# Dots of the matrix memory in buffers of their own, and the order at the ends of two MLPs

## The chip, the cores and the metric

The kernel runs on one core of one Trainium2 chip. The metric is the device time of one execution in microseconds (us); of several runs the median is given. A profiled execution leaves a trace, from which the profile's views are made. Engines in these views: PE is TensorE (PEld its weight loads), DVE is VectorE, ACT is ScalarE, POOL is GpSimd, SP is SyncE, which here issues nearly all DMAs.

## What is computed

A trunk of four residual sub-layers over a sequence of 1024 tokens with 1024 channels, in float32. Cut to what matters here:

```python
for i in range(DEPTH):                      # DEPTH = 2
    mod = c_act @ mod_w[i] + mod_b[i]       # six rows of 1024: shifts, scales, gates
    sh_a, sc_a, g_a, sh_f, sc_f, g_f = [t[:, None, :] for t in jnp.split(mod, 6, axis=-1)]
    h = rms_norm(x) * (1 + sc_a) + sh_a
    y = mla_mixer(h, ...) if i % 2 == 0 else mlstm_mixer(h, ...)
    x = x + g_a * y
    h = rms_norm(x) * (1 + sc_f) + sh_f
    x = x + g_f * conv_ffn(h, ffn_w_up[i], ffn_conv_w[i], ffn_conv_b[i], ffn_w_down[i])
return rms_norm(x, final_norm)

def conv_ffn(h, w_up, conv_w, conv_b, w_down):        # D_FF = 2816
    a, g = jnp.split(h @ w_up, 2, axis=-1)
    a = causal_depthwise_conv3(a, conv_w) + conv_b
    return (jax.nn.gelu(a, approximate=False) * g) @ w_down
```

`mla_mixer` is latent attention with 8 heads. `mlstm_mixer` is the matrix memory, with 4 heads: queries, keys, values, an output gate, and two scalar gates per token and head. The scalar gates give running sums and maxima, from which the decay between tokens comes; the memory is then updated chunk by chunk:

```python
num = inter_w * (C @ q) + ((q @ k.T) * exp(dmat - m)) @ v
C_new = decay * C + (ws * v).T @ k
```

## The kernel before

**Precision and tiling.** Channels lie on the 128 partitions, tokens along the free axis in two halves of 512. Each float32 operand of a large product is split into a high and a low part (type fp32r): ACT copies the source to the high part, DVE or POOL subtracts it from the source to get the low part. One product is then three matmuls, high by high, low by high and high by low (`mm3`, lines 175 to 177). A weight of 128 x 512 or 128 x 1024 is loaded by SP into a raw buffer (`wraw` or `raw`), split into `whi` and `wlo`, and used. `wp` holds four buffers of 1024 columns for the parts (in an MLP eight places of 512) and two called `wraw`.

**Who sets the order.** The program is written as a list of instructions for each engine. A planner (the Tile framework's scheduler) takes them in order of priority, which is their place in the text, and issues on each engine the first that its own model of the chip holds to be ready. So an instruction can float ahead of its place in the text if its inputs and buffers are there, and the order on each engine is fixed when the kernel is built. `tc.high_priority()` moves what is inside it forward; `tc.keep_in_program_order(i)` forbids `i` to overtake the instruction that was written before it on the same engine. On the chip, each engine then works its list strictly in order. `later(n, fn, key)` is a counter in the text: `fn` is written after `n` more `mm3`, or when `need(key)` asks for it.

**Modulation rows.** The six rows of a layer are dots of `mod_w` with silu(c), done on DVE: `mod_dot` (line 198), 128 x 1024 elements with an accumulator, after a load of 512 KB. `mod_steps` is a generator that loads and dots one row block per step, 8 per row; `piece(mods, n)` runs `n` steps. In the matrix memory three rows of the second layer, (1, 2), (1, 4) and (1, 3), are made: 24 steps, two for each of the four parts of the values of the second, third and fourth head (`v_proj`), in raw buffers from `wraw`, each dot written directly behind its load.

**The matrix memory.** First the values of head 0 with the scalar gates' columns (`vp`), then `qk(1)`, the queries and keys of head 1, run while the gates are worked out in four steps, `gates0` to `gates3`, on DVE and ACT with small transposes on PE (`gg`, `gr`, `gp`, `gcol`), written after 2, 16, 20 and 24 `mm3` (`GATES`). `piece(nxt, QK1)` writes 20 `mm3`, and `need(gcol)` then writes the rest. `load_rows` brings the gates' rows back through DRAM; `prep` makes the decayed score matrix `pT` and the weighted queries and keys for a half; `chain` runs the eight chunks, with `po` and `pc` as PSUM tiles. Projections of the next head or of the output gate (`inp`, `vp`) are written between the chunks as cover. After the chain of head 1, `qk(2)` is written, and after that of head 2, `qk(3)`, with `finish`, the head's transposes (`yT`).

**The MLP.** Both products of an MLP, up and down, are cut in halves of the tokens, of the inner channels and of the output rows, with sums and differences of operands and weights, so that seven half products replace eight. The operands are B11, B21, T1, B22, T2, T3 and T4; T1 to T4 are differences, made by DVE and split. The up-projection has 22 groups of 7 steps; a step is four `mm3`. Steps 1 and 2 need only the first half of the normalised input, the others the second. The first four groups (`AHEAD`) run steps 1 and 2 first, because the second half's operands come late; T2, T3 and T4 are written by hooks after steps 7, 8 and 10 of the list (`REST`). `LOOK` says how many steps ahead of its use a weight's preparation is written. Steps 6, 7 and 4 of a group add to the same PSUM bank `A` as step 1, and DVE reads the bank between them (lines 1073, 1080 and 1039). The results go to DRAM (`ud`) and come back as operands of the down-projection, which has three groups of 28 steps; its four U operands take the places of T operands that are done. Hooks at the last steps of the up-projection (`ends`) load these, the residual stream x, and close the pool of the up-projection (`turn`), whose place the second half of the down weights (`raw1`, loaded from `wd`) takes.

**Statistics before an MLP.** `out_proj` sums the squares of x by DVE and ACT. `X_WAIT` `mm3` after the end of a half, PE sums them over the partitions (`st`, line 254), DVE and POOL take the root; `X_RSTD` `mm3` after that PE spreads the result over rows (`rb`, line 266), and the operands can be made (line 915 on).

## Time and profile before

| | |
|---|---|
| median of 3 runs | 2213.28 us |
| lowest and highest | 2211.96 and 2214.94 us |
| the profiled execution, around its span | 2209.6 us |
| its span, first to last instruction | 2207.8 us |
| granted TensorE clock over the span | 0.996 |
| ACT busy | 1045.3 us (47%) |
| POOL busy | 200.5 us (9%) |
| HBM read and written over the span | 221.53 and 44.47 MB |

A row of a group in the profile has the line, engine and operation, then output <- input by the program's names, the shape, the count, and behind the bar the busy time in us and the mean of one in ns; behind the second bar stands the idle time of the engine just before these instructions and what ended it. A row of a timeline begins with the start and the duration in us; a bracket at its end has the idle time before it. A row of the list of waits has the total in us, how often, and the longest. A row of a table of stages has the stage, its length, then busy us and count for PE, PEld, DVE, ACT and POOL, the granted clock, the share of the DMA engines and GB/s. Matmuls are pipelined: one takes about 0.39 us from start to end, and the next starts some 0.23 us after it.

### The profile page before, as it was taken

How to read it: one execution, taken by the hardware profiler on the slowest of the kernel's cores; microseconds unless marked ns; L12 is line 12 of the kernel's file. 1: busy time of each engine (PE TensorE's matmuls, PEld its weight loads, DVE VectorE, ACT ScalarE, POOL GpSimd, SP SyncE). 2: the span in 40 equal slices, each digit the busy share in tenths (PEclk: the TensorE clock that was granted, in tenths of full speed). 3: DMA queues.
4: the chain of work that ended last, by engine and by line, in shares of the span. 5: the costliest groups of instructions: out<-in, count | busy, mean ns of one | idle time of the engine just before them, and what ended most of it. 6: DMA issues, size and time to landing. Idle time of an engine off the chain costs nothing.

```text
span 2207.8 us, 28744 instructions
## 1 busy us (share of the span) xinstructions
PE 2165.6 (98%) x10557; PEld 1817.1 (82%) x10557; DVE 1697.9 (77%) x2753; ACT 1045.3 (47%) x1812; POOL 200.5 (9%) x232
## 2 busy tenths in 40 slices
PE   9999999999999999999999999999999999999998
PEld 7878888787888888778888888988788888877887
DVE  8877788669878776999974754566887777779987
ACT  6456566456444444443353434354554444453335
POOL 0000000000000000242210111010000000022232
PEclk9999999999999999999999999999999999999999
DMA  8512334832444432543133332354233332245122
GB/s 316 156 47 67 94 102 156 278 115 74 151 143 138 134 130 80 191 150 95 51 115 105 102 124 77 114 172 158 68 134 100 110 116 95 78 155 208 45 79 77
DMA packets 105085, 270.50 MB, mean 123 GB/s; under 512 B 12336, under 2 KB 15984, under 8 KB 104944
## 3 DMA queue, kind: packets, MB, share of 16 engines
q1 hardware_dynamic: 104544, 268.28, 36.8%
q8 instruction: 83, 1.36, 0.2%
q14 instruction: 58, 0.48, 0.1%
q10 hardware_dynamic: 400, 0.39, 0.1%
HBM read 221.53 MB, written 44.47 MB: 120 GB/s over the span
## 4 chain that ended last, share of the span: by engine, by line
PE 85%; DVE 8%; DMA 2%; ACT 2%; issue 1%; POOL 0%; SPq 0%; DVEq 0%; POOLq 0%; ACTq 0%
PE pa L177 7%; PE pa L175 7%; PE pa L176 7%; PE pd L175 4%; PE pd L176 4%; PE pd L177 4%; PE sc L677 3%; PE da L175 3%; PE da L177 3%; PE da L176 3%; PE op L175 3%; PE op L177 2%; PE op L176 2%; PE inp L177 2%; PE inp L175 2%; PE db L177 2%
## 5 line engine op out<-in xcount | busy, mean ns | idle before, releaser
L992 ACT ACTIVATE whi<-raw 128x512 fp32r<-128x512 f32 (+1 forms) x252 | 147.5, 607 | 262.3 <-PE pb L176 61.0
L992 ACT ACTIVATE whi<-wsum 128x512 fp32r<-128x512 f32 (+1 forms) x224 | 133.9, 617 | 184.5 <-PE pa L176 61.5
L175 PE MATMUL pa<-T,whi 128*128 128x512 f32 x528 | 206.3, 391 | 5.0 <-DVE g L1080 5.0
L177 PE MATMUL pa<-T,wlo 128*128 128x512 f32 x528 | 206.1, 390 | 3.1 <-DVE wlo L993 3.1
L176 PE MATMUL pa<-T,whi 128*128 128x512 f32 x528 | 205.7, 390 | 0.0
L993 DVE TENSOR_TENSOR wlo<-wsum,whi 128x512 fp32r<-128x512 f32 (+1 forms) x224 | 150.6, 685 | 33.7 <-ACT whi L992 32.2
L993 POOL TENSOR_TENSOR wlo<-raw,whi 128x512 fp32r<-128x512 f32 (+1 forms) x96 | 140.8, 1480 | 382.5 <-ACT whi L992 341.8
L175 PE MATMUL da<-U,whi 128*128 128x512 f32 (+1 forms) x364 | 139.8, 384 | 2.2 <-ACT whi L992 2.2
L176 PE MATMUL da<-U,whi 128*128 128x512 f32 (+1 forms) x364 | 139.2, 382 | 0.0
L177 PE MATMUL da<-U,wlo 128*128 128x512 f32 (+1 forms) x364 | 138.5, 382 | 0.0
L167 ACT ACTIVATE whi<-wraw 128x1024 fp32r<-128x1024 f32 x67 | 70.7, 1058 | 112.7 <-PE op L176 60.2
L993 DVE TENSOR_TENSOR wlo<-raw,whi 128x512 fp32r<-128x512 f32 (+1 forms) x156 | 104.7, 678 | 24.4 <-ACT whi L992 24.4
L175 PEld LDWEIGHTS pa<-T,whi 128*128 128x128 f32 x528 | 99.3, 188 | 28.0 <-DVE g L1080 4.1
L177 PEld LDWEIGHTS pa<-T,wlo 128*128 128x128 f32 x528 | 99.3, 188 | 24.5 <-DVE wlo L993 4.0
L176 PEld LDWEIGHTS pa<-T,whi 128*128 128x128 f32 x528 | 99.3, 188 | 20.4
L1143 DVE TENSOR_TENSOR U<-q,U 128x1024 fp32r<-128x1024 f32 x84 | 108.2, 1306 | 6.0 <-ACT U L1142 5.5
L1032 ACT ACTIVATE ct<-a,cols 128x512 f32<-128x512 f32 x88 | 71.0, 808 | 87.5 <-DVE a L1054 47.8
L168 DVE TENSOR_TENSOR wlo<-wraw,whi 128x1024 fp32r<-128x1024 f32 x67 | 82.4, 1233 | 37.0 <-ACT whi L167 34.9
L177 PE MATMUL db<-U,wlo 128*128 128x512 f32 x264 | 102.7, 390 | 1.7 <-DVE wlo L993 1.7
L175 PE MATMUL db<-U,whi 128*128 128x512 f32 x264 | 103.7, 393 | 0.0
L176 PE MATMUL db<-U,whi 128*128 128x512 f32 x264 | 102.8, 390 | 0.0
L175 PE MATMUL op<-oh,whi 128*128 128x512 f32 x256 | 100.1, 391 | 1.0 <-ACT oh L731 1.0
(378 smaller groups left out, 6078.5 us busy)
## 6 DMA issues: line engine op xcount, KB each, us to landing
raw<-in_wf SPq DMA_DIRECT2D x96, 512.0 KB, 4.1
wraw<-in_w SPq DMA_DIRECT2D x67, 512.0 KB, 3.6
mraw<-in_mod_w SPq DMA_DIRECT2D x56, 512.0 KB, 3.6
ud<-ct SPq DMA_DIRECT2D x88, 256.0 KB, 2.3
q<-ud SPq DMA_DIRECT2D x88, 256.0 KB, 4.1
raw<-in_wd SPq DMA_DIRECT2D x32, 512.0 KB, 5.7
pa<-in_mod_w SPq DMA_DIRECT2D x24, 512.0 KB, 3.6
x<-xd SPq DMA_DIRECT2D x48, 256.0 KB, 4.4
```

The source lines that it names most:

```text
L167: act.activation(hi, raw, AF.Copy)
L168: dve.tensor_tensor(lo, raw, hi.bitcast(F32), ALU.subtract)
L175: pe.matmul(ps, lh, rh, start=first, stop=False, skip_group_check=more)
L176: pe.matmul(ps[:, 0:rl.shape[-1]], lh, rl, start=False, stop=False, skip_group_check=more)
L177: pe.matmul(ps, ll, rh, start=False, stop=last, skip_group_check=more)
L677: pe.matmul(ps[:, cs], a[:, qs if n < 3 else qrs_], b[:, cs], start=n == 0, stop=n == 4)
L992: act.activation(hi, src, AF.Copy)
L993: eng.tensor_tensor(lo, src, hi.bitcast(F32), ALU.subtract)
L1032: act.activation(t, a[:, 2:], AF.Identity, bias=col(f"cb{l}", m), scale=cw(m, 2))
L1143: dve.tensor_tensor(lo, w, hi.bitcast(F32), ALU.subtract)
```

## The change

- `GATES` goes from (2, 16, 20, 24) to (2, 18, 22, 26).
- `mod_steps` now writes every dot one step after its load, and pinned behind what was written before it on DVE; before, this held for the steps without a row `c` of their own, and the matrix memory's dots stood directly behind their loads. Their raw buffers are two of a pool of the matrix memory (`MRAWS`), no longer `wraw`. The steps move from `v_proj` of heads 1 to 3 to `qk(2)` and `qk(3)`: two and one in each half of each projection, 12 for each head.
- `X_WAIT` and `X_RSTD` of the second half go from 4 to 3.
- In the first eight steps of an MLP the weights are written 7 ahead instead of 5.
- In the first four groups the order 5, 4, 5, 4 of two pairs becomes 5, 5, 4, 4.
- `out` of step 4 (the product with the gate, and its store) gets high priority.
- In the first group of the down-projection the low parts of the weights of B11 and B21 are made by DVE instead of POOL.
- The last step 4 of the up-projection moves behind the first two steps of the down-projection, and with it, two places later, `turn` and the loads of x for the first half.

```diff
-GATES = (2, 16, 20, 24)
+GATES = (2, 18, 22, 26)
...
-AHEAD, LOOK, RAWS = 4, 5, 5
-X_WAIT, X_RSTD = (12, 4), (8, 4)
+AHEAD, LOOK, RAWS, MRAWS = 4, (7, 5), 5, 2
+X_WAIT, X_RSTD = (12, 3), (8, 3)
...
                 nc.sync.dma_start(raw, mod_w[l, j * 8 + k])
-                if c is None:
-                    yield
-                    tc.keep_in_program_order(mod_dot(l, j * 8 + k, raw))
-                else:
-                    mod_dot(l, j * 8 + k, raw, c)
-                    yield
+                yield
+                tc.keep_in_program_order(mod_dot(l, j * 8 + k, raw, c))
...
         def p4(g, w):
             prod(g["A"], w, "T4", False)
-            out(g, 0, g["t1"], g["A"])
+            with tc.high_priority():
+                out(g, 0, g["t1"], g["A"])
...
-            seq += [(k, g) for g in pair] if k != (5, 4) else [(5, b[0]), (4, a[0]), (5, b[1]), (4, a[1])]
+            seq += [(k, g) for g in pair] if k != (5, 4) else [(5, b[0]), (5, b[1]), (4, a[0]), (4, a[1])]
...
-                return wop(weights(g, p, 0)[op == "B21"], pool)
+                return wop(weights(g, p, 0)[op == "B21"], pool if g else dve)
...
-        hook(ends[4], turn)
-        hook(ends[4], lambda: load_x_tiles(0))
+        hook(ends[4] + 2, turn)
+        hook(ends[4] + 2, lambda: load_x_tiles(0))
...
+        e = ends[4]
+        seq[e:e + 3] = [*seq[e + 1:e + 3], seq[e]]
         ws = []
         for i, (_, run_) in enumerate(seq):
-            while len(ws) < len(seq) and len(ws) <= i + LOOK:
+            while len(ws) < len(seq) and len(ws) <= i + LOOK[i >= 2 * AHEAD]:
...
             for hf in range(2):
-                yield from in_steps(u, hf, lambda ps: qk_evac(ps, t, hf, scale))
+                for n, _ in enumerate(in_steps(u, hf, lambda ps: qk_evac(ps, t, hf, scale))):
+                    if hd > 1:
+                        piece(mods, 2 - n)
+                    yield
...
             split_ps(va[0][:, 2 * t2:2 * t2 + 2, 0:256], va[1][:, 2 * t2:2 * t2 + 2, :], ps3)
-            piece(mods, 2)
             yield va
...
-                     lambda: wp.tile([P, 1024], F32, tag="wraw", bufs=wraws, name=nm("mraw")), crow2)
+                     lambda: pm.tile([P, D], F32, tag="mraw", bufs=MRAWS, name=nm("mraw")), crow2)
```

## The prediction

> **What bounds the kernel now.** I read the first part of the page, and then the table of stages of 50 us.
>
> ```profile
> span 2207.8 us, 28744 instructions
> ...
> PE 2165.6 (98%) x10557; PEld 1817.1 (82%) x10557; DVE 1697.9 (77%) x2753; ACT 1045.3 (47%) x1812; POOL 200.5 (9%) x232
> ...
> 500.00:550.00 50.00, 47.58 (x209) 38.77 (x208) 49.71 (x71) 31.67 (x48) 0.10 (x1) 1.00 0.23 68
> ...
> 650.00:700.00 50.00, 50.00 (x223) 41.40 (x222) 40.29 (x66) 22.56 (x38) 0.30 (x3) 1.00 0.45 151
> ...
> 1200.00:1250.00 50.00, 45.41 (x280) 39.10 (x279) 38.73 (x102) 22.31 (x59) 7.75 (x9) 1.00 0.49 153
> ```
>
> TensorE is busy 2165.6 of 2207.8 us, so a change that takes away no matmul can win at most the 42.2 us in which it idles. In a stage without holes it does 223 matmuls in 50 us, one per 0.225 us; one weight block against one operand block, three matmuls (`mm3`), takes 0.67 us, and a step of the MLP (four of them) 2.7 us. In each row the first pair after the length is PE, the third DVE. Two kinds of hole show: stages where DVE is nearly full (49.71 of 50), and the matrix memory's first head (45.41), where DVE is not full and something is late. The diff touches both kinds. It removes no matmul and adds none.
>
> **The matrix memory.** Three holes, by the list of waits between 1186 and 1240 us, and the DVE timeline at two of them:
>
> ```profile
> PE po L177 <- DVE pT L1405: 2.3, 1, 2.3
> PE gr L1567 <- DVE crow L1563: 2.1, 1, 2.1
> ...
> PE po L175 <- ACT pT L1404: 0.9, 1, 0.9
> ...
> 1198.22 1.21 DVE L198 SCALAR_TENSOR_TENSOR mraw<-mraw,crow 128x1024 f32<-128x1024 f32 x1
> ...
> 1199.37 0.41 DVE L1563 TENSOR_TENSOR_SCAN crow<-crow 32x128 f32<-32x128 f32 x1
> ...
> 1200.76 0.17 DVE L1575 COPY mprow<-mend 1x28 f32<-1x28 f32 x1
> ...
> 1219.57 1.21 DVE L198 SCALAR_TENSOR_TENSOR mraw<-mraw,crow 128x1024 f32<-128x1024 f32 x1
> ...
> 1222.29 0.68 DVE L1405 TENSOR_TENSOR pT<-crow,pT 128x512 fp32r<-128x512 f32 x1
> ```
>
> L198 is the dot of a modulation row. In the text it belongs to the second head's values, but the planner has floated it forward: it stands directly ahead of the scan that the gates wait for, and between 1219.57 and 1222.29 (there are two) ahead of the low part of pT that `po` waits for. After the change no dot is written before the third head's queries, and each is pinned behind the DVE instruction traced before it, so none can stand here.
>
> - Hole of 2.1 (`gr`): without the dot the scan starts at 1198.22, 1.15 us sooner; GATES puts `gr` two `mm3` later, 2 x 0.67 = 1.35 us that TensorE works meanwhile. 1.15 + 1.35 = 2.5 > 2.1: it goes. The third and fourth gate step move as well, but the end of `piece(nxt, QK1)`, 20 `mm3`, already brings the rest; `gp` now follows `gr` after two `mm3` instead of four. What it needs, L1575, ends at 1200.93, 1.15 us after the scan's end at 1199.78 with `gr` between them; two `mm3` take 1.35, so I cost that at nothing, and at 1.15 if they did not cover it.
> - Hole of 2.3 (pT low): 1222.29 - 1219.57 = 2.72 us of dots go. 2.72 > 2.3: it goes.
> - Hole of 0.9 (pT high): the chain is sooner by 1.15 at the scan and by up to 1.35 at `gp`, 2.5 in all, and TensorE arrives 2.1 sooner. What is left of the gain is about 0.4; I take 0.5, the middle of the ends 0 and 0.9.
>
> Sum: -(2.1 + 2.3 + 0.5) = **-4.9 us**; ends -5.3 and, if the scheduler floats other DVE work into the freed places so that only the hole at `gr` goes, about -2.0.
>
> What it adds: the same 24 dots and 24 loads, 12 for each of the third and fourth head, in `qk`. The stage of the third head's queries and keys:
>
> ```profile
> 1300.00:1324.00 24.00, 24.00 (x124) 20.43 (x123) 13.67 (x20) 4.29 (x6) 1.56 (x1) 1.00 0.54 175
> ...
> L198 DVE SCALAR_TENSOR_TENSOR mraw<-mraw,crow x6: 1212/1223/1226, 1299.9 to 1315.1; 128x1024 f32<-128x1024 f32 x6
> ...
>   DMA mraw<-in_mod_w: 14.0, 12
> ```
>
> TensorE is full there, DVE 13.67 of 24 with six dots in it already; six more are 6 x 1.22 = 7.3 us, within the 10.3 free. (The last row counts what DVE waited for landings ahead of all 24 dots.) The loads go through two buffers of their own, so the weights' loads no longer queue behind dots for `wraw`. Cost: nothing, as long as TensorE's projection covers it (the second rival prices it without that cover).
>
> **Start of each MLP.** PE and DVE timelines of the first one, ACT's last square, a table of one stage, and two rows of the list of waits of the whole span:
>
> ```profile
> 485.56 0.63 ACT L233 ACTIVATE sq<-x 128x512 f32<-128x512 f32 x1
> ...
> 487.24 0.28 PE L254 MATMUL st<-ones,ssq 128*128 128x1 f32 x2
> ...
> 489.12 0.16 DVE L258 TENSOR_SCALAR var<-st 128x4 f32<-128x4 f32 x1 [2.45 <-PE st L254]
> 492.06 0.69 DVE L1054 TENSOR_TENSOR a<-a,pb 128x512 f32<-128x512 f32 x1 [2.78 <-PE pb L177]
> ...
> 514.29 2.35 DVE L922 TENSOR_TENSOR T<-o,T 128x1024 fp32r<-128x1024 f32 x2
> ...
> 519.48 0.39 PE L175 MATMUL pa<-T,whi 128*128 128x512 f32 x1
> ...
> 528.67 0.47 PE L175 MATMUL pa<-T,whi 128*128 128x512 f32 x1 [0.87 <-DVE g L1080]
> ...
> 530.92 0.50 PE L177 MATMUL pa<-T,wlo 128*128 128x512 f32 x1 [1.55 <-DVE wlo L993]
> ...
> 492.10:553.70 61.60, 59.18 (x261) 48.38 (x260) 61.31 (x84) 40.30 (x60) 0.10 (x1) 1.00 0.25 76
> ...
> PE pa L175 <- DVE g L1080: 5.0, 4, 1.7
> PE pa L177 <- DVE wlo L993: 3.1, 2, 1.5
> ```
>
> DVE starves (2.45 and 2.78 us) until the statistics of the second half arrive, then works 61.31 of 61.60 us, and TensorE loses 0.87 + 1.55 = 2.4 us inside that stretch. So the stretch is DVE's, and its start decides. X_WAIT and X_RSTD bring the statistics one `mm3` sooner and the turn to rows one more: L915, whose work opens the stretch, starts 2 x 0.67 = 1.35 us sooner. The inputs allow it: the last square ends at 486.19, and the statistics would start at 487.24 - 0.67 = 486.57. In a full stretch each microsecond sooner is one less of waiting, up to 2.4: -1.35 per MLP, **-2.7 us** for two: the waits of the second kind are 3.1 in two places, so the second MLP shows the same.
>
> The rest here adds no operation. LOOK of 7 writes three weights ahead of T2's operands, about 2.1 us of DVE (three low parts and a sum, each near the 678 ns of the group L993 below); T2 is done at 516.64 and first read at 519.48, so 2.8 us of slack hides it, and without it up to 2.1 would show. The order (5, 5, 4, 4) gives TensorE something else to do while T4 is late, but step 5's weight comes off the same full DVE at the same time as the weight that step 4 waited for. I take 0; bounds -1.05 (the rest of the 2.4) and +1.0 per MLP.
>
> **End of each MLP's up-projection.** The list of waits between 880 and 1000 us, the table of one stage, the groups of the low parts on DVE and on POOL, and DVE groups in 890:960 against 600:850:
>
> ```profile
> PE pa L175 <- DVE g L1080: 1.7, 1, 1.7
> PE da L175 <- ACT whi L992: 1.1, 2, 0.6
> PE db L177 <- DVE wlo L993: 0.8, 1, 0.8
> ...
> 903.60:959.20 55.60, 53.09 (x229) 41.87 (x228) 55.45 (x67) 21.17 (x30) 10.42 (x6) 1.00 0.58 198
> ...
> L993 DVE TENSOR_TENSOR wlo<-raw,whi 128x512 fp32r<-128x512 f32 (+1 forms) x156 | 104.7, 678 | 24.4 <-ACT whi L992 24.4
> ...
> L993 POOL TENSOR_TENSOR wlo<-raw,whi 128x512 fp32r<-128x512 f32 x64 | 103.3, 1628 | 295.7 <-ACT whi L992 255.0 <-DVE U L1143 35.3 <-PE da L177 5.3
> ...
> L1033 DVE SCALAR_TENSOR_TENSOR ct<-a,cols,ct 128x512 f32<-128x512 f32 x2 | 3.0, 1488 | 0.0
> ...
> L1039 DVE TENSOR_TENSOR ct<-ct,g 128x512 f32<-128x512 f32 x2 | 2.3, 1168 | 0.0
> ...
> L1033 DVE SCALAR_TENSOR_TENSOR ct<-a,cols,ct 128x512 f32<-128x512 f32 x27 | 20.2, 747 | 3.5 <-ACT ct L1032 3.5
> ...
> L1039 DVE TENSOR_TENSOR ct<-ct,g 128x512 f32<-128x512 f32 x13 | 9.0, 689 | 0.2
> ```
>
> The hole of 1.7 is the last step 4, which waits for DVE to take step 7's result out of the same bank. The change puts two steps of the down-projection (5.4 us) ahead of it, so this wait goes. But DVE works 55.45 of 55.60 us from 903.6 to 959.2, through that hole and the next (the 0.8 on `db`): TensorE that arrives 1.7 us sooner at `db` finds DVE where it was. What is late next is that low part, by 1.7 more. Unless DVE's work there shrinks, nothing is won.
>
> Does it? Eight low parts per MLP (B11 and B21 of the first group) go from POOL to DVE: 8 x 0.68 = 5.4 us more, about half of it after 903.6. Against it, DVE operations are long where POOL works beside them: L1033 by 0.74 us and L1039 by 0.48, about 0.6 a part, 8 x 0.6 = 4.8 us that go away, again spread over both halves. 5.4 - 4.8 = +0.6, half of it in the full stretch. That is small beside the rest of the stretch, and I take **0** per MLP; bounds +2.7 (no relief, half of 5.4) and -3.6 (all three waits go).
>
> The Trainium skill, page "SBUF — State Buffer", section "Who interferes with whom", has a DVE instruction with two SBUF inputs and a GpSimd instruction that reads SBUF exclude each other for the whole instruction. By that rule eight POOL parts could hold DVE for 8 x 1.63 = 13 us, and moving them would free 7.6 us per MLP. By the rows the trace agrees only in part: 0.6 us a part, not 1.63; the third rival carries the rest.
>
> The moved `turn` and `load_x_tiles(0)`: eight x loads, and behind them on SP's queue the wd loads for T1.
>
> ```profile
> 921.23 2.22 SPq L1155 DMA_DIRECT2D raw<-in_wd  x4
> ...
> 928.50 1.28 DVE L1166 TENSOR_TENSOR wsum<-raw 128x512 f32<-128x512 f32 x2
> ...
> raw<-in_wd SPq DMA_DIRECT2D x32, 512.0 KB, 5.7
> ```
>
> Before, the wd loads start at 921.23, as soon as the x loads are out; the first lands about 921.2 + 5.7 = 926.9, used at 928.5: 1.6 us of slack. Step 4 is moved by two steps, 5.4 us, less the 1.7 that it no longer waits and what the planner runs ahead of it already: at most 3.7 us later, against 1.6 of slack. I take nothing, because part of the two steps does run ahead of it, at worst +2.1 per MLP. `out` of step 4 at high priority is one DVE operation sooner and keeps the store, and with it `turn`, from drifting.
>
> **Sum.** -4.9 - 2.7 + 0 = -7.6 us. The profiled execution took 2209.6 us around its span of 2207.8, and would take 2202.0; the median of the runs shown is 2213.28, 3.7 above it, so I give **2205.7**.
>
> **Rivals.**
> 1. DVE's full stretches take it back: the moved low parts bring no relief (+2.7 per MLP), while the starts and the memory give what I forecast. -4.9 - 2.7 + 5.4 = -2.2, 2211.1 us: not to be told from no change. For it: 55.45 of 55.60. Against: the long L1033 and L1039.
> 2. Slower: the pinned dots hold DVE. A dot whose row has not landed stops everything behind it on DVE: the low parts of weights, then `prep` and `chain` of the next head. Before, 12 such waits took 14.0 us, 1.17 each. If all 24 wait so, DVE needs 12 x (1.22 + 1.17) = 28.7 us beside the 6 us of other work in a stage of 24 us: 10.7 over per head, 21.4 in all. Should all of it reach TensorE: -7.6 + 21.4 = +13.8, 2227.1 us. It decides from about 12 us on. Against it: before, those waits fell where TensorE stayed full (24.00 of 24.00), and a row has a buffer to land in while the other is worked on.
> 3. POOL's release pays in full: the three waits at each transition go (1.7 + 1.1 + 0.8 = 3.6 per MLP, 7.2 in all): 2205.7 - 7.2 = 2198.5 us. For it: 1488 against 747 ns. Against: the 1.1 is two waits on ACT's whi, not on POOL.
> 4. The scheduler floats other work into the freed places, the memory gives -2.0 alone: 2208.6, inside the first case's range.
>
> **Chances.** Forecast with rival 4: 0.55 (2202 to 2209). Rival 1: 0.21. Rival 2: 0.08. Rival 3: 0.16. Forecast and rival 3 lie below 2208.9, so faster by over 0.2% (about what a measurement of this kernel can tell from no change): 0.71. Within: rival 1, 0.21. Slower: rival 2, 0.08. The range takes in rivals 3 and 1 and leaves out rival 2: 2198.5 to 2212.
>
> **What would show it.** Memory right: no L198 on DVE before about 1290, and the list of waits at 1186 to 1240 without `gr` <- L1563 and `po` <- L1405. Start right: L915 begins 1.35 us sooner after the last `op` matmul, and the two waits together are near 1 us instead of 2.4. Transition right: the wait on L1080 is gone and those on `db` and `da` have grown by about as much, with DVE still full. Wrong: DVE waits for `mraw` and TensorE for DVE in the third and fourth head (rival 2), or transitions without any wait (rival 3).

## The result, and the profile after

| kernel | median us | executions | ratio to the kernel before, 95% interval |
|---|---|---|---|
| before, beside it | 2214.11 | 6 | |
| changed | 2196.92 | 6 | 0.9923 [0.991, 0.9936] |
| changed, measured again | 2196.77 | 5 | 0.9932 [0.992, 0.9945] |

The change is faster by 17.2 us, 0.77%. The forecast was 2205.7, with a range of 2198.5 to 2212: the time lies below the range. The sign was right, and the gain is more than double the forecast 7.6 us.

The first rows of the changed kernel's page, and from its list of TensorE's waits over the whole span (total us, how often, longest) those rows of 1 us and more that belong to the places of the prediction:

```profile
span 2194.9 us, 28739 instructions
...
PE 2164.6 (99%) x10557; PEld 1818.9 (83%) x10557; DVE 1692.5 (77%) x2769; ACT 1049.7 (48%) x1812; POOL 175.2 (8%) x216
```

```profile
PE da L177 <- DVE wlo L989: 2.0, 2, 1.0
...
PE pd L175 <- ACT whi L988: 1.9, 2, 1.0
...
PE po L176 <- DVE C L1475: 1.6, 3, 0.6
PE po L175 <- ACT C L1474: 1.6, 3, 1.0
...
PE db L175 <- ACT whi L988: 1.3, 2, 0.6
```

Line numbers are up to 4 off those of before: L989 was L993, L1035 was L1039, L1140 was L1143, L1475 was L1473. Before, the list was led by `pa` <- `g` L1080 with 5.0 us in four places; that wait is gone everywhere. The span is 12.9 us shorter than that of the one profiled execution before, but the medians are 17.2 apart. The row to keep in mind for what follows is DVE: it is busy 1692.5 us against 1697.9, although it made 16 more low parts.

**Memory, after.** Waits of TensorE from 1186 to 1240, then DVE (three rows) and TensorE (one) at the scan:

```profile
PE po L175 <- ACT pT L1406: 0.7, 1, 0.7
PE po L175 <- ACT C L1474: 0.3, 1, 0.3
PE po L176 <- DVE C L1475: 0.3, 1, 0.3
```

```profile
1195.05 0.28 DVE L1564 TENSOR_TENSOR crow<-crow 32x128 f32<-32x128 f32 x1
1195.36 0.41 DVE L1565 TENSOR_TENSOR_SCAN crow<-crow 32x128 f32<-32x128 f32 x1
...
1197.59 0.17 DVE L1577 COPY mprow<-mend 1x28 f32<-1x28 f32 x1
```

```profile
1198.11 0.17 PE L1582 MATMUL gp<-ident,mprow 1*32 1x1 f32 x1
```

No dot stands ahead of the scan: it starts where its input ends (1195.33). Neither `gr` nor `po` <- pT low is in the list, and `gp` runs 0.35 us after its input is there, without a wait of its own. Before, the list had two small rows more than the prediction showed:

```profile
PE po L176 <- DVE C L1473: 0.8, 1, 0.8
PE po L175 <- ACT C L1472: 0.6, 1, 0.6
```

With these, five waits of 6.7 us have become three of 1.3.

**Start and end of an MLP, after.** DVE's first row of the full stretch; the same stretches as before in the tables of stages; DVE's groups from 890 to 960:

```profile
491.81 2.35 DVE L911 TENSOR_TENSOR x<-x,rb 128x1024 f32<-128x1024 f32 x2 [2.46 <-PE rb L262]
```

```profile
492.10:553.70 61.60, 60.50 (x264) 48.77 (x263) 61.31 (x85) 42.23 (x63) 0.10 (x1) 1.00 0.25 88
```

```profile
903.60:959.20 55.60, 53.96 (x236) 43.76 (x235) 55.16 (x71) 20.55 (x30) 2.98 (x2) 1.00 0.60 206
```

```profile
L989 DVE TENSOR_TENSOR wlo<-raw,whi 128x512 fp32r<-128x512 f32 x13 | 8.8, 685 | 0.0
...
L1029 DVE SCALAR_TENSOR_TENSOR ct<-a,cols,ct 128x512 f32<-128x512 f32 x2 | 1.5, 745 | 0.0
L1035 DVE TENSOR_TENSOR ct<-ct,g 128x512 f32<-128x512 f32 x2 | 1.4, 685 | 0.0
```

Both stretches are still DVE's (61.31 of 61.60, 55.16 of 55.60), yet TensorE gets through 264 instead of 261 matmuls in the first and 236 instead of 229 in the second. At the start, L911 (L915 before) begins 6.4 us after the end of the last `op` matmul, before 8.0: 1.6 sooner, where 1.35 was forecast. The two waits of 2.4 us have become two of 1.1 (`pd`, on whi and on wlo; 1.2 in the second MLP). At the end, POOL works 2.98 us in the stretch, not 10.42, and the `ct` operations that took 1488 and 1168 ns take 745 and 685, the usual time. TensorE's waits there went from 3.6 to 1.8 us (3.5 to 1.8 in the second MLP): the one on `g` is gone, and the two others of before, 1.9 us, have become three of 1.8:

```profile
PE da L177 <- DVE wlo L989: 1.0, 1, 1.0
PE db L175 <- ACT whi L988: 0.6, 1, 0.6
PE da L175 <- DVE x L294: 0.2, 1, 0.2
```

### The profile page after: what moved, and what is told of

Its sections match the earlier page's. It is cut to its first block, busy times and chain, and to the rows that moved or that the text cites. A ratio compares the mean times of both kernels' runs of the same rounds, so it can differ in the third digit from the quotient of the medians.

```text
span 2194.9 us, 28739 instructions
## 1 busy us (share of the span) xinstructions
PE 2164.6 (99%) x10557; PEld 1818.9 (83%) x10557; DVE 1692.5 (77%) x2769; ACT 1049.7 (48%) x1812; POOL 175.2 (8%) x216
## 4 chain that ended last, share of the span: by engine, by line
PE 84%; DVE 9%; DMA 2%; ACT 2%; issue 2%; POOL 0%; SPq 0%; DVEq 0%; POOLq 0%; ACTq 0%
PE pa L175 7%; PE pa L177 7%; PE pa L176 7%; PE sc L673 3%; PE pd L177 3%; PE pd L175 3%; PE pd L176 3%; PE db L175 3%; PE db L176 3%; PE db L177 3%; PE op L175 3%; PE op L176 3%; PE op L177 3%; PE da L175 2%; PE da L176 2%; PE da L177 2%
## 5 line engine op out<-in xcount | busy, mean ns | idle before, releaser
L989 DVE TENSOR_TENSOR wlo<-wsum,whi 128x512 fp32r<-128x512 f32 (+1 forms) x224 | 151.5, 692 | 33.0 <-ACT whi L988 31.6
L989 POOL TENSOR_TENSOR wlo<-raw,whi 128x512 fp32r<-128x512 f32 (+1 forms) x80 | 116.3, 1467 | 401.2 <-ACT whi L988 398.7
L989 DVE TENSOR_TENSOR wlo<-raw,whi 128x512 fp32r<-128x512 f32 (+1 forms) x172 | 116.1, 681 | 24.9 <-ACT whi L988 24.9
L1140 DVE TENSOR_TENSOR U<-q,U 128x1024 fp32r<-128x1024 f32 x84 | 102.7, 1239 | 10.3 <-ACT U L1139 9.8
L175 PE MATMUL inp<-h,whi 128*128 128x512 f32 x256 | 100.9, 395 | 0.0
```

Of the source, the lines that this page charges most:

```text
L175: pe.matmul(ps, lh, rh, start=first, stop=False, skip_group_check=more)
L989: eng.tensor_tensor(lo, src, hi.bitcast(F32), ALU.subtract)
L1140: dve.tensor_tensor(lo, w, hi.bitcast(F32), ALU.subtract)
```

## Experiments

Ratios are to the kernel before, measured beside it on the same chip, with a 95% interval; "us" is (ratio - 1) x 2213. Where a stage is compared, the time between the same two TensorE instructions (by their count, 10557 in all) is taken from both traces, so that the rest of the kernel doesn't matter. This table is worked out from the traces in that way; it gives each stage's time less that of the first profiled execution of before, in us.

| kernel | MLP 1 start (486 to 870) | MLP 1 end (870 to 1090) | memory (1180 to 1300) | memory (1300 to 1450) | MLP 2 start (1560 to 1930) | MLP 2 end (1930 to 2110) |
|---|---|---|---|---|---|---|
| before, again | +1.4 | +0.2 | +2.2 | +1.0 | -0.2 | -0.2 |
| memory alone | +1.6 | 0 | -5.1 | +2.7 | -1.6 | 0 |
| ends alone | +1.3 | -1.9 | +1.5 | 0 | -0.1 | -2.8 |
| low parts alone | +1.5 | -0.7 | +0.7 | +2.7 | 0 | -2.8 |
| order of the ends alone | 0 | +1.0 | +2.1 | +0.7 | -1.6 | +0.1 |
| starts alone | -1.0 | 0 | +1.4 | +0.6 | -2.6 | 0 |
| statistics alone | -1.5 | +0.1 | +1.9 | +0.8 | -3.1 | 0 |
| changed | -1.0 | -2.9 | -5.2 | +0.7 | -2.6 | -3.0 |
| changed, again | -1.0 | 0 | -5.8 | 0 | -2.7 | -1.3 |
| no POOL parts, weights 9 ahead | -1.4 | -4.5 | -5.8 | +0.8 | -3.0 | -5.3 |

Stages that an edit doesn't touch differ by up to 2.7 us between executions: by half-clock stretches of TensorE, to which the section on the hardware comes back, and from 1300 to 1450 also by TensorE's wait on C, which was 0.6 us in the first profile of before, 1.4 in the second and 1.5 in that of the low parts alone. In the start of the second MLP the execution of before that all are compared with has a stretch of half clock at 1598, so up to 1.7 us of the -1.6, -2.6 and -3.1 there are that stretch.

### The kernel before, once more

No edit.

> The kernel before, unchanged, profiled once more. The profiled execution of before took 2209.6 us, 4.5 below the median of its six runs, while that of the change lies 0.3 from its median. Theory A: that execution was a short one of the same program; this one has a span near 2212 and the difference to the first is spread over the whole span or lies in one place that waits for DMA. Rival B: a profile costs nothing and the span is 2208 again; then the runs' 17.2 us hold about 4 us that no profiled execution shows.

Measured 2212.24 us, ratio 1.000 [0.999, 1.001]. Its profiled execution has a span of 2213.1, 5.3 above the one that the prediction was made from: that one was at the fast end of the kernel's own spread. As far as the table shows, the difference lies in the places where this execution has half-clock stretches and the first has none (531, 1204 and 1228), and in the wait on C.

### The three parts

The memory: the hunks on `GATES`, `mod_steps`, `qk`, `v_proj` and `mods`. The ends: the hunks on `d_w`, `hook(ends[4] + 2, ...)` and `seq[e:e + 3]`. The starts: those on `LOOK`, `X_WAIT`, the order 5, 5, 4, 4 and `out`. Each is the diff of the change cut to these lines, the first of each:

```diff
-GATES = (2, 16, 20, 24)
+GATES = (2, 18, 22, 26)
...
-                return wop(weights(g, p, 0)[op == "B21"], pool)
+                return wop(weights(g, p, 0)[op == "B21"], pool if g else dve)
...
-X_WAIT, X_RSTD = (12, 4), (8, 4)
+X_WAIT, X_RSTD = (12, 3), (8, 3)
```

> Only the matrix memory's part: the dots in two buffers of their own, pinned and moved to the third and fourth head's queries and keys, and the gates' places. Theory: the holes at the gates and at the first two products of the chain go, 5.5 us by the matmul counts of the two traces (1150 to 1250 us); ratio 0.9975. Rival: the part also carries what the runs show beyond the traces (17.2 against 12.9); then 9 to 10 us, ratio 0.9955.

> Only the end of each up-projection: the low parts of the first group on DVE, the last step 4 two steps later with its hooks. Theory: POOL's release of DVE is worth about 1 us a part against 0.68 that the part costs, DVE's busy time falls by about 5 us in all, and each MLP wins 2.8 us: 5.6, ratio 0.9975. Rival (my prediction): DVE stays full and gives the hole back at the next product, 0 to 1 us, ratio 1.000.

> Only the start of each MLP: statistics sooner, weights 7 ahead, the order 5, 5, 4, 4, step 4's product at high priority (this last one acts in all groups). Theory: 1.0 us per MLP, 2.1 in all, ratio 0.999. Rival: the high priority shortens other waits on DVE in the groups' steady state too, 4 us or more, ratio 0.998.

| part | median us | ratio | us | forecast |
|---|---|---|---|---|
| memory | 2207.72 | 0.9977 [0.9968, 0.9986] | -5.1 | -4.9 |
| ends | 2206.66 | 0.9969 [0.9958, 0.9981] | -6.9 | 0 |
| starts | 2209.02 | 0.9982 [0.9972, 0.9991] | -4.0 | -2.7 |

Each interval is 4 to 5 us wide. The three add up to -16.0, within that of the whole change's -17.2, so nothing shows that the parts touch each other. Of the 9.6 us that the forecast missed, 6.9 are the ends.

### The ends: POOL or the order

The first run moves the low parts only, the second the last step 4 with `turn` and the x loads only.

```diff
-                return wop(weights(g, p, 0)[op == "B21"], pool)
+                return wop(weights(g, p, 0)[op == "B21"], pool if g else dve)
```

```diff
-        hook(ends[4], turn)
-        hook(ends[4], lambda: load_x_tiles(0))
+        hook(ends[4] + 2, turn)
+        hook(ends[4] + 2, lambda: load_x_tiles(0))
...
+        e = ends[4]
+        seq[e:e + 3] = [*seq[e + 1:e + 3], seq[e]]
```

> Before, with one part alone: the low parts of B11 and B21 of the down-projection's first group on DVE instead of POOL (8 an MLP); turn, the x loads and the last step 4 stay where they were. It splits the 6 to 7 us that the two edits at the end of the up-projection gave together. Theory POOL: each part that leaves POOL frees about 1.0 us of DVE and costs it 0.68, so DVE's busy time falls by about 5 us in the span, and the edit alone gives -3 to -6 us: about 2208 to 2210. The wait of step 4 on DVE (g, 1.7 us an MLP) stays. Theory order (the one of the prediction): the relief is 0.6 a part, DVE's busy time stays within 1 us, and the edit alone gives 0, within 1.5 us of the kernel before.

> Before, with the other half of that pair alone: the last step 4 of the up-projection behind the first two steps of the down-projection, with turn and the x loads two places later; the low parts stay on POOL. Theory POOL: DVE is as full as before, so TensorE only meets it later; the wait on g goes and those on wlo and whi at da and db grow by about 1.7 us an MLP: 0, within 1.5 us. Theory order: the 1.7 us an MLP are won whatever POOL does: -3.4 us. If the two edits need each other, both runs give less than half of the 6.9 us of the pair.

Low parts alone: 2209.61, ratio 0.9986 [0.9976, 0.9995], -3.1 us. Order alone: 2214.45, 1.001 [1.0, 1.002], +2.2. Both: -6.9. The engine rows of the pages of, in this order, the kernel before again, the order alone, the low parts alone and both:

```profile
PE 2171.0 (98%) x10557; PEld 1821.2 (82%) x10557; DVE 1698.9 (77%) x2753; ACT 1045.3 (47%) x1812; POOL 200.5 (9%) x232
```

```profile
PE 2165.5 (98%) x10557; PEld 1816.5 (82%) x10557; DVE 1699.3 (77%) x2753; ACT 1048.1 (47%) x1812; POOL 199.0 (9%) x232
```

```profile
PE 2170.2 (98%) x10557; PEld 1823.0 (82%) x10557; DVE 1693.7 (77%) x2769; ACT 1049.4 (47%) x1812; POOL 177.2 (8%) x216
```

```profile
PE 2168.2 (98%) x10557; PEld 1822.2 (83%) x10557; DVE 1692.4 (77%) x2769; ACT 1046.3 (47%) x1812; POOL 176.2 (8%) x216
```

DVE has 16 instructions more in the last two (2769 against 2753) and is busy 5 to 7 us less. One low part on DVE takes 0.68 us, so 16 add 10.9; DVE's other work has become 16 to 18 us shorter, 1.0 to 1.1 us for each part that left POOL. The order does nothing to DVE.

The place where this reaches TensorE is the wait on `g`. DVE takes step 6's result out of the bank at L1073 and step 7's at L1080, which is when `g` is there. Before, on DVE and then on POOL:

```profile
904.17 2.21 DVE L1141 TENSOR_TENSOR q<-q,q 128x1024 f32<-128x1024 f32 x1
906.31 1.78 DVE L1033 SCALAR_TENSOR_TENSOR ct<-a,cols,ct 128x512 f32<-128x512 f32 x1
...
909.82 0.68 DVE L1080 TENSOR_TENSOR g<-g,pa 128x512 f32<-128x512 f32 x1
```

```profile
904.02 3.53 POOL L993 TENSOR_TENSOR wlo<-raw,whi 128x512 fp32r<-128x512 f32 x2 [2.39 <-ACT whi L992]
```

With the low parts alone:

```profile
907.19 0.68 DVE L993 TENSOR_TENSOR wlo<-raw,whi 128x512 fp32r<-128x512 f32 x1
907.80 1.22 DVE L1141 TENSOR_TENSOR q<-q,q 128x1024 f32<-128x1024 f32 x1
908.93 0.75 DVE L1033 SCALAR_TENSOR_TENSOR ct<-a,cols,ct 128x512 f32<-128x512 f32 x1
...
910.83 0.68 DVE L1080 TENSOR_TENSOR g<-g,pa 128x512 f32<-128x512 f32 x1
```

Two parts on POOL make two DVE operations 2.0 us longer. One low part (0.6 us from start to start) takes their place there, and L1034 (0.7) now comes after L1080, so that `g` is there 4.9 us after L1073 starts instead of 7.0 (4.8 instead of 7.0 in the second MLP). The wait on `g` is gone with the low parts alone, which neither theory expected. TensorE's time from 903.6 to 930, and over the same place in the second MLP, is 1.9 to 2.0 us shorter in the profiles of the low parts alone, of both, and in the two of the changed kernel: 3.9 us for the two MLPs.

What the order does alone is in its waits from 880 to 1000 us:

```profile
PE da L175 <- DVE ct L1039: 1.6, 1, 1.6
PE db L177 <- DVE wlo L993: 1.4, 2, 0.9
PE da L175 <- ACT whi L992: 1.1, 2, 0.6
```

The wait on `g` is gone, and a wait of the same 1.6 us has come in its place: `da` takes the bank that step 4's `out` reads, and now waits for that read. It is the prediction's "TensorE that arrives 1.7 us sooner at `db` finds DVE where it was". The theory called POOL gave the order alone 0, within 1.5 us; +2.2 is beyond that on the slow side. Together the two win more than the sum of both alone (-0.9). That the two edits need each other isn't shown: the intervals are 4 to 5 us wide, and in the second MLP the profile of the low parts alone wins as much as that of both (-2.8).

### No low part on POOL

```diff
-                return wop(weights(g, p, 0)[op == "B21"], pool if g else dve)
+                return wop(weights(g, p, 0)[op == "B21"], dve)
...
-                return wop(weights(g, p, 1)[1], pool)
+                return wop(weights(g, p, 1)[1], dve)
...
-                       pool if op == "T3" else dve)
+                       dve)
```

> The changed kernel with no low part of the down-projection on POOL at all: the 80 that were left there go to DVE. It asks whether the relief of about 1.0 us a part holds for the others too. Relief 1.0 everywhere: DVE's busy time falls by 80 x 0.3 = 24 us, to about 1668, and since most of these parts lie where TensorE is full, the time falls by 0 to 3 us: 2194 to 2197. Relief only where DVE has no slack of its own (POOL shares little of its time with a busy DVE): DVE's busy time rises by up to 80 x 0.68 = 54 us, to about 1745, and the stages where DVE has 2 to 5 us free fill up: 2197 to 2205.

2192.9 us, ratio 0.991 [0.9891, 0.9928]. From 880 to 1000 us, TensorE has no wait left that the list shows. Neither expectation on DVE held, and the time is below both their ranges: DVE's busy time rose to 1701.0, by 8.5, so 80 more parts cost it about 0.1 each, a relief near 0.57 a part.

The relief can also be read off operation by operation: each DVE operation that overlaps a low part on POOL, less the median of the same operation in the fastest version without POOL parts (below). So counted, the 96 parts of before lengthen DVE by 50 us, 0.52 a part, and the 80 of the changed kernel by 35 to 36. The eight parts that the change moves lengthen it by 4.6 to 5.6 us in each MLP, 0.58 to 0.70 a part. Most of the rest of the 1.0 to 1.1 above is the parts that stayed, which lengthen DVE less than before: in the first MLP 15.4 to 17.0 us instead of 18.6, in the second 10.5 to 11.1 instead of 13. Why they do isn't shown.

How POOL holds DVE up shows best in the second run of the changed kernel, on DVE and on POOL, and in the group of the same operation from 880 to 1080 in the fastest version:

```profile
986.41 1.65 DVE L1140 TENSOR_TENSOR U<-q,U 128x1024 fp32r<-128x1024 f32 x1
987.98 2.31 DVE L1138 TENSOR_TENSOR q<-q,q 128x1024 f32<-128x1024 f32 x1
...
991.91 2.31 DVE L1138 TENSOR_TENSOR q<-q,q 128x1024 f32<-128x1024 f32 x1
```

```profile
983.42 9.72 POOL L989 TENSOR_TENSOR wlo<-raw,whi 128x512 fp32r<-128x512 f32 x5 [2.78 <-ACT whi L988]
```

```profile
L1138 DVE TENSOR_TENSOR q<-q,q 128x1024 f32<-128x1024 f32 x10 | 12.1, 1214 | 0.2 <-DMA q<-ud 0.2
```

Five low parts in a row on POOL, 1.94 us each, and the difference that takes 1214 ns takes 2310. Behind it TensorE waits 1.5 us for DVE's x (L294), and that execution's first MLP end won nothing (the table above): what the other parts on POOL take back there differs from execution to execution. The Trainium skill, page "SBUF — State Buffer", section "Who interferes with whom", has the two engines exclude each other on a shared port; a delay of 1.1 us on one operation beside POOL parts of 1.94 agrees with it in kind, while the mean over the 96 parts of before, 0.52, doesn't reach a part's length.

### The memory without GATES

All hunks of the memory but the first; against the run with the memory alone:

```diff
-GATES = (2, 18, 22, 26)
+GATES = (2, 16, 20, 24)
```

> Before, with the matrix memory's dots moved to the queries and keys of the third and fourth head, pinned, in two buffers of their own, and GATES left at (2, 16, 20, 24). The forecast's steps: the scan starts 1.15 us sooner, so of the hole of 2.1 us at gr 0.95 stays; the holes of 2.3 and 0.9 at pT stay gone or nearly so. By that it gives -3.5 us, against -5.1 with GATES. Rival: the dots are all of it and GATES nothing, because the planner, with no dot to float there, puts gr where its inputs are: -5, no wait on L1563. Other rival: the planner floats other DVE work into the freed place: the hole at gr stays near 2, -2 to -3 in all.

2207.93 us, ratio 0.9984 [0.9974, 0.9994], -3.5. Its list of waits from 1180 to 1240:

```profile
PE gr L1565 <- DVE crow L1561: 0.9, 1, 0.9
PE po L175 <- ACT pT L1402: 0.8, 1, 0.8
```

The step was 2.1 - 1.15 = 0.95, and 0.9 is there, so the dots are the main thing and `GATES` takes the rest. Both rivals fall by this list; the medians alone, 1.6 us apart, couldn't tell.

### The start: statistics or order

```diff
-X_WAIT, X_RSTD = (12, 4), (8, 4)
+X_WAIT, X_RSTD = (12, 3), (8, 3)
```

```diff
-AHEAD, LOOK, RAWS = 4, 5, 5
+AHEAD, LOOK, RAWS = 4, (7, 5), 5
...
-            seq += [(k, g) for g in pair] if k != (5, 4) else [(5, b[0]), (4, a[0]), (5, b[1]), (4, a[1])]
+            seq += [(k, g) for g in pair] if k != (5, 4) else [(5, b[0]), (5, b[1]), (4, a[0]), (4, a[1])]
...
-            out(g, 0, g["t1"], g["A"])
+            with tc.high_priority():
+                out(g, 0, g["t1"], g["A"])
```

> Before with the statistics of the second half sooner (X_WAIT and X_RSTD 3 instead of 4) and nothing else of the start. Theory of the prediction: DVE's full stretch opens 1.35 us sooner in each MLP, and the two holes at its end (1.0 and 1.7 us) shrink by that much together: -2.7 us, about 2209.5. Rival: the holes at 529 to 531 are a matter of what DVE does just ahead of the weight, not of when the stretch began; then the stretch opens sooner, the holes stay within 0.3 us of 1.0 and 1.7, and the time is the same within 1 us.

> Before with the other part of the start: weights 7 ahead in the first eight steps, the order 5, 5, 4, 4, and out at high priority; the statistics as they were. Theory of the prediction: 0, within 2 us, the holes at 529 to 531 stay about 2.7 together. Rival: the order alone takes the hole of 1.7 us away (TensorE has a step 5 to do while step 4's operand is late), so the two together fall to about 1.1 and the time by 3.4 us; then the part with the statistics should give nothing beside it.

Statistics alone: 2208.98, ratio 0.9982 [0.9973, 0.9991], -4.0 us. The other part alone (weights 7 ahead, the order, `out` at high priority): 2209.06, 0.9988 [0.9979, 0.9997], -2.7. Waits from 495 to 560, first with the statistics, then with the order:

```profile
PE pd L175 <- ACT whi L992: 0.9, 1, 0.9
```

```profile
PE pd L177 <- DVE wlo L993: 0.9, 1, 0.9
PE pd L175 <- ACT whi L992: 0.4, 1, 0.4
```

Of the 2.4 us of before, 0.9 is left by the one and 1.3 by the other; with both, 1.1. The theory of the full stretch holds for the statistics: the stage is 1.5 us shorter in the first MLP (forecast 1.35). The order alone takes the two waits to 1.3, near what the rival named (1.1) and not the prediction (2.7); its stage is 0.6 us shorter in each MLP. Beside the statistics it wins nothing: the stage is 1.0 shorter with both, 1.5 with the statistics alone. The medians can't order the two parts, since their intervals overlap.

### Filling a hole

To see whether a hole costs more than its length, matmuls that nobody reads were put into the one at `gr`: 16, and then 8, because one of float32 took two passes of 0.109 us and 16 held `gr` up.

```diff
         ps = px("gr")
+        for _ in range(FILL):
+            tc.keep_in_program_order(pe.matmul(ps[:, 0:P], ident, ident, start=True, stop=True))
```

> Before with 16 matmuls of 128 x 128 of the identity with itself, written into the bank of gr ahead of its transposes, so that TensorE works through most of its hole of 2.1 us at 1200 (16 x 0.109 = 1.7 us). The result of these is overwritten; nothing else is changed, and the hole's end stays where DVE's scan puts it. Theory clock: the hole costs more than its length, because the granted clock is halved for about 3.4 us behind a window with much idle time (1.7 us of loss, in about three of four executions of before there); filled, there is no half clock between 1198 and 1210 in the profile, the mean granted clock rises by about 0.0005, and the time falls by about 1.3 us although 16 matmuls were added. Theory idle time: only the length of the hole counts; the time is the same, or up to 0.3 us longer, and the mean clock is that of before, 0.9935.

> As the run with 16 filling matmuls ahead of gr, with 8: of float32, one took two passes of 0.109 us, so 16 took 3.6 us and held gr up by 1.4; 8 take 1.75 and end inside the hole of 2.1. Theory clock: no half clock between 1198 and 1210 in the profile, and the median 0.5 to 1.3 us below the kernel before, with a mean clock 0.0003 to 0.0007 above its 0.9935. Theory idle time: the time is that of before within 0.5 us, and so is the mean clock.

2214.68 us, ratio 1.0011 [1.0002, 1.002], with 16; 2212.45, 0.9999 [0.999, 1.0007], with 8. In both profiles the clock stays full through 1200 to 1208, and in both a half-clock stretch stands behind the next hole, at 1224.4 and 1221.6. The run with 8 doesn't answer the question either. Its -0.2 us have an interval from -2.2 to +1.5, which takes in what the theory of the clock forecast (-0.5 to -1.3) and what the theory of idle time did. And its idle time isn't less: the planner's order came out another way, with 20 instead of 36 matmuls of the projections (`inp`) ahead of the first `po`, so that from 1186 to 1240 TensorE waits 4.5 us at once for pT on ACT, 1.3 for C and 0.9 for `gcol`, 6.7 in all, as much as before. Whether a hole costs more than its length stays open.

### A version that beats the changed kernel

Weights 9 instead of 7 ahead on top of the kernel without POOL parts, twice, and that version without the moved step 4; the changed kernel ran beside the last two.

```diff
-AHEAD, LOOK, RAWS, MRAWS = 4, (7, 5), 5, 2
+AHEAD, LOOK, RAWS, MRAWS = 4, (9, 5), 5, 2
```

```diff
-        hook(ends[4] + 2, turn)
-        hook(ends[4] + 2, lambda: load_x_tiles(0))
+        hook(ends[4], turn)
+        hook(ends[4], lambda: load_x_tiles(0))
...
-        e = ends[4]
-        seq[e:e + 3] = [*seq[e + 1:e + 3], seq[e]]
```

> The kernel without low parts on POOL (2192.9 us, -19.4 against before), and weights 9 instead of 7 ahead in the first eight steps of an MLP. It asks whether the hole of 1.1 us that is left at 529 and 1588 (step 5 of the third group, waiting for its whi) is only an order on DVE, T's differences ahead of the weight's sum. If so it shrinks, up to -2.2 us: 2190.7 to 2193. If the full stretch as a whole decides, T2's operands come later by what the weights take (about 1.4 us more) and the hole moves to where they are first read: 2193 to 2196.

> The changed kernel, unchanged, as the measure for the other two of this call: 2196 to 2198 us, ratio 0.9925.

> The kernel without low parts on POOL and with weights 9 ahead, once more, beside the changed kernel: if what the single looks showed holds, 2190 to 2192 us, 5 to 7 us below the changed kernel; if that was the luck of four executions, within 2 us of it.

> The kernel without low parts on POOL and with weights 9 ahead, with the last step 4, turn and the x loads where they were before. Alone, moving them lost about 2 us. Theory: the move only pays when DVE isn't full: without it the wait on g of 1.7 us an MLP is back and nothing else, so +3.4 against the version with the move, about 2194. Rival: relieved of POOL, DVE takes step 7's result out in time and the move is worth nothing or less: 2189 to 2191.

| kernel | median us | ratio |
|---|---|---|
| weights 9 ahead, first | 2190.64 | 0.9903 [0.9889, 0.9916] |
| changed | 2196.77 | 0.9932 [0.992, 0.9945] |
| weights 9 ahead, again | 2188.72 | 0.9895 [0.9882, 0.9909] |
| the same without the moved step 4 | 2189.41 | 0.9895 [0.988, 0.991] |

It beats the changed kernel, which ran beside it, by 8 us. Most of that is POOL: the two ends are 4.5 and 5.3 us shorter than before, those of the changed kernel beside it 0 and 1.3. What the 9 itself brings is within the noise; the hole that it was meant for moved from 529 to 535 and is as long (1.0). The moved step 4 is worth nothing here: the rival held. Relieved of POOL, DVE has step 7's result out of the bank in time, as it had with the low parts alone.

## Why the prediction fell short

- **Memory, -4.9: right**, step by step: -5.1, with an interval of 4 us. The dot ahead of the scan cost 1.15, `GATES` the other 0.95, and `gp` nothing. Of the third hole 0.7 is left instead of 0.4, and two small waits on C shrank that weren't counted. What was costed at nothing shows no cost: from 1280 to 1420 DVE waits 18.5 us for 13 landings of `mraw`, and still TensorE is full in the stage with the dots (25.00 of 25.00). That is the second rival's mechanism without its effect. To the microsecond it can't be told, since the time from 1300 to 1450 differs by 2.7 us without moved dots too (the table above). The first dot comes at 1262.5, sooner than the 1290 that was named, with the queries of the third head.

```profile
  DMA mraw<-in_mod_w: 18.5, 13
```

```profile
1300.00:1325.00 25.00, 25.00 (x156) 22.62 (x155) 12.91 (x22) 4.29 (x6) 0.00 (x0) 1.00 0.70 231
```

- **Starts, -2.7: the mechanism right.** L911 begins sooner and the waits shrink, as forecast. The size can't be told: by the stages it is 1.0 us an MLP in the changed kernel, once a stretch of half clock in the second is taken off, which is less than the 1.35; by the median it is -4.0, with an interval from -6.2 to -2.0 that takes in the forecast. The order, costed at 0 with a bound of -1.05, gives 0.6 alone and nothing beside the statistics.
- **Ends, 0: the failed step.** It is the sum "5.4 - 4.8 = +0.6, half of it in the full stretch". The 4.8 was near: the eight parts lengthen DVE by 4.8 and 5.4 us in the profile of before. What failed is that cost and relief were spread evenly over the stretch, so that DVE's work there seemed not to shrink. TensorE's wait hangs on DVE's way from L1073 to L1080. There two POOL parts cost 2.0 us, and one low part of 0.6 came in for them, with L1034 moved behind. `g` came 2.0 us sooner, and TensorE gained 1.9 to 2.0 in each MLP at that place, with the order or without it. The sign that the prediction named, "those on `db` and `da` have grown by about as much", shows the same: they went from 1.9 to 1.8. A second thing wasn't in the sum: the parts that stay on POOL lengthen DVE less than before, 4 to 6 us in all. A row that would have warned of them was there: the 84 low parts of the down-projection's operands (L1143, later L1140) took 1306 ns on average before, 1239 after, and 1128 in the fastest version without POOL parts; little of their lengthening lies beside the eight.

  The place at L1080 accounts for 3.9 of the 6.9 us of the ends. The other 3 stay open: behind it, the profiles of kernels with these ends lie between 1.9 us slower and 1.0 faster than before in one MLP, so that the 2.9 and 3.0 of the changed kernel's first profile (0 and 1.3 in its second) are partly luck. The rest of the step held: without relief, TensorE meets DVE where it was (the order alone, +2.2). The moved `turn` cost nothing, as taken: the wd loads start at 919.6 instead of 921.2. The third rival's 2198.5 came near the time, but not by its mechanism: of its three waits only the one on `g` went.
- **From span to median, +3.7: a number from one execution.** It isn't a term of the gain, since 2205.7 is the old median less 7.6 either way; but it says that 2207.8 was an unusually short span. In the 17 later profiles, the profiled execution lies between 1.4 us below and 3.2 above the median of its kernel's runs, and no other is as far below as that one. The changed kernel's first lies at its median and its second 3.2 above. So the 12.9 us between the two spans are too few, by a chance of which execution was profiled.
- **What had no term.** The mean granted clock rose by 0.0018, which would stand for about 2.2 us (below). The prediction has nothing for it.

## What to carry to other kernels

Price a part on POOL by where the operations stand that it lengthens, not by its mean over a stretch. By the mean (0.6 us a part against 0.68 for making it on DVE) the move was worth nothing; on the way to the one result that TensorE waited for, it freed 2.0 us for 0.6. DVE's total doesn't tell it either: without any part on POOL, DVE is busy 8.5 us longer than in the changed kernel, and the kernel is no slower. So follow the engine from the last thing it waited for to the result that is waited for, and count what is lengthened and what is added on that way. And before a median is derived from one profile, ask where that execution lies in the kernel's own spread.

## What the runs showed of the hardware

**POOL beside DVE.** In the first profile of before, 99 DVE operations that read both operands from SBUF overlap a low part on POOL; they are 0.50 us longer on average than the same operation in the fastest version, which has no POOL parts, and up to 1.1. Another 68 that overlap one read one operand from PSUM (`pa`, `pb`, `da`, `db`); they are not longer (0.00 us on average, 0.01 at most). The second profile of before has the same counts and means.

**The clock.** Between 200 and 2150 us, the granted clock drops to half for stretches of 3.41 us (3413 ns in the clock's record), and which holes are followed by one differs between executions of the same kernel. Tables of stages around the hole at `gr`, of the kernel before run again and of its first profiled execution (columns: stretch, us, PE busy and count, granted clock, DMA share, GB/s):

```profile
1200.00:1202.00 2.00, 0.11 (x1) 1.00 0.01 4
...
1203.00:1204.00 1.00, 1.00 (x6) 0.86 0.84 180
1204.00:1205.00 1.00, 1.00 (x4) 0.50 0.69 283
1205.00:1206.00 1.00, 1.00 (x4) 0.50 0.14 33
1206.00:1207.00 1.00, 1.00 (x5) 0.50 0.80 315
```

```profile
1198.00:1200.00 2.00, 0.17 (x3) 1.00 0.02 4
1200.00:1202.00 2.00, 2.00 (x11) 1.00 0.62 190
```

The same hole is followed by half clock in one and by full clock in the other. A stretch can cost 3.41 / 2 = 1.7 us (an estimate, for a TensorE that is busy all the time). The clock's record has 1 such stretch in the first profile of before, 4 in the second, 3 and 3 in the two with a filled hole; 1 and 1 in the two of the changed kernel; none in three of the four without POOL parts. The mean granted clock over the 104 executions of the kernel before that ran with the experiments is 0.9935; it is 0.9953 and 0.9954 over 6 and 5 of the changed one and 0.9962 over 4 of the fastest version. Among the 104, a clock lower by 0.001 goes with a span longer by 1.2 us, so 0.0018 would stand for about 2.2 us of the gain. That holes set these stretches off isn't shown. Most stand close behind a wait of 1.5 us or more, but the one of the changed kernel, at 1129, stands behind 16 narrow matmuls (`st`, one column each) with no wait over 0.31 us; and the filling experiment, which might have told, left as much idle time as before.

The Trainium skill, page "TensorE: Matmul & The Clock Gate", section "What's actually happening", has a free-running window of 3413 ns, which the record's length agrees with, and a clock that halves after an idle window of about that length. Here the idle time ahead of the stretch shown is 2.1 us; so if idle time is what sets it off, a window that is only partly idle was enough.
